# Moving 24 conditioning columns of the first attention to TensorE, with a third load buffer and new scheduling priorities

## The chip, the cores and the metric

The kernel runs on one core of a Trainium2 chip. A core has five engines that work side by side, each on its own instructions in their written order: TensorE (PE; PEld is its weight load), VectorE (DVE), ScalarE (ACT), GpSimd (POOL) and SyncE (SP), which here only issues transfers. The metric is the time of one execution in microseconds (us), the median of several runs; lower is better.

## What is computed

Two transformer layers over 512 tokens of 1024 features, in float32. Both layers are steered by a conditioning vector `c`: a product with a 1024 x 6144 matrix gives six vectors of 1024 per layer (a shift, a scale and a gate for the attention, the same for the MLP). Cut to what matters:

```python
c_act = silu(c)
for l in range(2):
    ada = c_act @ ada_w[l] + ada_b[l]                 # 6 x 1024 numbers
    sh1, sc1, g1, sh2, sc2, g2 = split(ada, 6)
    h = x * (1 + sc1) + sh1
    y = even_mixer(h) if l == 0 else diff_mixer(h)    # attention
    x = layer_norm(ALPHA * x + (1 + g1) * y)
    h = x * (1 + sc2) + sh2
    x = layer_norm(ALPHA * x + (1 + g2) * square(relu(h @ w1)) @ w2)
```

The first attention (`even_mixer`) has two groups of heads: eight with three branches (compressed, selected and window keys; below, the first heads), and eight on a latent of rank 128 with an index that keeps 256 keys for each query (the second heads). The conditioning of layer 0 is 48 columns of 128 numbers: columns 0 to 15 are needed before the first projection, 16 to 23 (the gate `g1`) before the output projection, 24 to 39 before the MLP, 40 to 47 at its end.

## The kernel before

All weights pass through one stream (`Stream`, from L107): a list of items in the order of their use. `issue` (L134) starts the transfer of the next item as soon as a raw buffer of 128 x 1024 floats is free. There are two such buffers for the whole program (`raw0`, `raw1`), four more at the start (`early`, two of them for the first 24 items only) and four in the MLPs. `prepare` then splits a weight into a high part (a rounding copy on ScalarE, L265) and the rest (a subtraction, L266, on DVE or POOL as the table `PLAN` says), since a product is made of three fast matmuls (`mm3`, L350 to L352). A raw buffer comes free when its item is prepared. The table's row `ord` gives the order of the items in the first attention; an `'a'` in it is one conditioning column.

A conditioning column in columns 0 to 39 of layer 0 is 128 outputs on the partitions by 1024 inputs: it is multiplied by `cact`, which holds the activated vector in every partition, and summed along the row. Columns 0 to 15 and three others do that in one DVE instruction (L250); the other 21 do the product on POOL (L247) and the sum on ScalarE (L248). `ada_bias` (L407) then adds the bias to eight columns on DVE. From column 40 on, and in layer 1, two columns come as a pair (`ada_pair`, L416): eight matmuls with 32 columns of weights each (L422), a copy by ScalarE (L425), two sums by a matmul with a selector (L427) and one addition on DVE (L428). A pair keeps its first raw buffer until the second is there, and one of the two PSUM banks of its tag ("mm" in the attention).

The first attention runs in slots. After the first projection (to about 71 us) the slots below 15 project further queries and keys, score the index (L504 and L505 on PE, a relu by ScalarE L1208, an accumulation by DVE L1164), normalise the latent (`latent`, L1102 to L1106 on DVE) and transpose it (`latent_t`, L1113 on PE). Then come 32 units of the first heads: scores (L504, L505), a maximum on DVE (L514), the exponential on ScalarE (L517), scaling on POOL (L1284), transposes (L1486), and the value products with the compressed part (`pv`, L1304 and L1312). Beside them DVE picks the largest index scores (L1190, L1191). Projections fill the gaps by estimated cost (`Fill`). The units of the second heads and the output projection follow.

The order on each engine is not the written one: a scheduler of the framework plays the program with its own durations and takes what is ready. `ahead(n)` raises the priority of what is made inside it, and `ahead(None)` gives it the highest there is; before, only the layer norms use it, with 0.

## Time and profile before

| | us |
|---|---|
| median of 3 runs | 1440.21 (1439.06 to 1440.84) |
| profiled execution | 1441.48 |
| its span, first to last instruction | 1439.40 |
| PE busy in it | 1338.4 |
| DVE busy in it | 1141.7 |
| ACT busy in it | 659.8 |
| POOL busy in it | 579.8 |

The span is what the trace shows; the execution's own time is 2.08 us more. Times of the trace count from the start of the span. The first attention takes about the first 372 us, the first MLP follows until about 800 us, the second attention until about 1065 us, and the second MLP to the end. A busy engine need not be the one that sets the end, and idle time of an engine costs nothing where others are later. "[idle before <-X]" behind a row names what the engine waited for.

### The profile page before, as it was taken

The page shows a single profiled execution, that of the slowest core. Times are in us where ns is not written, and L with a number is a line of the kernel's source. Part 1 is how long each engine was busy: PE and PEld are TensorE (multiplying, and loading weights), DVE is VectorE, ACT ScalarE, POOL GpSimd, SP SyncE. Part 2 cuts the span into 40 slices and gives each one's busy share as a digit, 9 for nine tenths or more (in the row PEclk, how much of TensorE's full clock was granted, in tenths as well). Part 3 has the DMA queues.
Part 4 walks back from the last instruction along what each step waited for, and adds up shares of the span by engine and source line. Part 5 has one row for each costly group of instructions (what it writes and reads, how often), then busy time and mean ns, then how long its engine had stood idle before and what let it go on. Part 6 is the DMA issues. An engine that isn't in the chain of part 4 may idle for free.

```text
span 1439.4 us, 22546 instructions
## 1 busy us (share of the span) xinstructions
PE 1338.4 (93%) x8286; PEld 1123.1 (78%) x8286; DVE 1141.7 (79%) x2186; ACT 659.8 (46%) x1412; POOL 579.8 (40%) x432
## 2 busy tenths in 40 slices
PE   6979799998899999999999799999979899999985
PEld 4868676676589888888887687887769789999974
DVE  7778979667569778877789925788976997888898
ACT  3555465746365423333332536776565443333321
POOL 1423577626432444444453721124164533122234
PEclk9989999899999999999999999999989999999997
DMA  9834323313731554544542442332450233323311
GB/s 353 288 116 142 116 89 118 119 58 118 263 117 46 175 191 162 183 169 161 191 161 94 144 164 88 103 103 76 152 163 6 91 100 118 106 72 117 117 59 59
DMA packets 58657, 189.52 MB, mean 132 GB/s; under 512 B 7794, under 2 KB 8498, under 8 KB 58548
## 3 DMA queue, kind: packets, MB, share of 16 engines
q1 hardware_dynamic: 55840, 184.67, 38.0%
q10 hardware_dynamic: 2708, 3.42, 0.7%
q8 instruction: 65, 1.06, 0.3%
q14 instruction: 44, 0.36, 0.1%
HBM read 178.42 MB, written 9.64 MB: 131 GB/s over the span
## 4 chain that ended last, share of the span: by engine, by line
PE 70%; DVE 19%; DMA 4%; issue 3%; ACT 2%; POOL 1%; DVEq 0%; SPq 0%; ACTq 0%; POOLq 0%
PE ps_mm L350 9%; PE ps_mm L351 9%; PE ps_mm L352 9%; PE ps_o L350 4%; PE ps_o L351 4%; PE ps_o L352 4%; PE ps_s L351 3%; PE ps_s L350 3%; PE ps_s L352 3%; PE ps_t L350 2%; PE ps_t L352 2%; PE ps_t L351 2%; PE ps_t L1486 2%; PE ps_s L504 2%; DVE u L738 2%
## 5 line engine op out<-in xcount | busy, mean ns | idle before, releaser
L350 PE MATMUL ps_mm<-hT,b 128*128 128x256 f32 (+1 forms) x560 | 188.9, 339 | 16.9 <-ACT b L265 13.2
L351 PE MATMUL ps_mm<-hT,b 128*128 128x256 f32 (+1 forms) x560 | 188.5, 337 | 5.2 <-DVE hT L724 5.1
L352 PE MATMUL ps_mm<-hT,b 128*128 128x256 f32 (+1 forms) x560 | 187.8, 336 | 1.8 <-DVE b L220 1.8
L350 PEld LDWEIGHTS ps_mm<-hT,b 128*128 128x128 f32 x560 | 107.6, 192 | 31.9 <-ACT b L265 13.2
L351 PEld LDWEIGHTS ps_mm<-hT,b 128*128 128x128 f32 x560 | 107.8, 193 | 17.8 <-DVE hT L724 5.6
L220 POOL TENSOR_TENSOR b<-s,b 128x512 fp32r<-128x512 f32 x33 | 46.6, 1415 | 184.6 <-ACT b L219 181.2
L517 ACT ACTIVATE z<-z,st 128x128 f32<-128x128 f32 (+3 forms) x160 | 89.3, 559 | 67.2 <-DVE st L514 61.3
L903 POOL TENSOR_TENSOR ot<-z,ot 128x512 fp32r<-128x512 f32 x39 | 61.3, 1573 | 142.0 <-ACT ot L902 128.4
L352 PEld LDWEIGHTS ps_mm<-hT,b 128*128 128x128 f32 x560 | 107.5, 192 | 11.4 <-DVE b L220 2.0
L350 PE MATMUL ps_o<-b,ot 128*128 128x512 f32 x251 | 101.2, 403 | 3.9 <-ACT b L265 2.2
L351 PE MATMUL ps_o<-b,ot 128*128 128x512 f32 x251 | 99.5, 397 | 3.0 <-DVE b L266 3.0
L738 DVE TENSOR_TENSOR u<-ps_o,u 128x512 f32<-128x512 f32 x121 | 82.4, 681 | 21.6 <-PE ps_o L352 21.2
L352 PE MATMUL ps_o<-b,ot 128*128 128x512 f32 x251 | 98.8, 394 | 0.0
L514 DVE CUSTOM_DVE_ANT_0 z<-ps_s,g 128x128 f32<-128x128 f32 (+3 forms) x160 | 75.0, 484 | 25.8 <-PE ps_s L505 23.6
L265 ACT CAST b<-raw 128x1024 fp32r<-128x1024 f32 (+1 forms) x62 | 64.5, 1043 | 65.9 <-issue 16.7
L266 DVE TENSOR_TENSOR b<-s,b 128x1024 fp32r<-128x1024 f32 x47 | 70.4, 1501 | 18.3 <-ACT b L265 17.9
L265 ACT CAST b<-s 128x1024 fp32r<-128x1024 f32 x47 | 49.1, 1049 | 77.6 <-DMA s<-mlp_w 18.9
L266 DVE TENSOR_TENSOR b<-raw,b 128x1024 fp32r<-128x1024 f32 (+1 forms) x42 | 56.7, 1349 | 33.1 <-ACT b L265 32.9
L350 PE MATMUL ps_s<-b,ot 128*128 128x512 f32 x181 | 72.4, 400 | 0.0
L738 DVE TENSOR_TENSOR u<-ps_s,u 128x512 f32<-128x512 f32 x87 | 59.3, 682 | 15.9 <-PE ps_s L352 15.6
L351 PE MATMUL ps_s<-b,ot 128*128 128x512 f32 x181 | 71.7, 396 | 0.0
L352 PE MATMUL ps_s<-b,ot 128*128 128x512 f32 x181 | 71.4, 394 | 0.0
(472 smaller groups left out, 4244.1 us busy)
## 6 DMA issues: line engine op xcount, KB each, us to landing
s<-mlp_w SPq DMA_DIRECT2D x55, 512.0 KB
s<-ada_p SPq DMA_DIRECT2D x39, 512.0 KB
s<-mlp_wp SPq DMA_DIRECT2D x33, 512.0 KB
raw<-ada_w SPq DMA_DIRECT2D x23, 512.0 KB
raw<-mlp_w SPq DMA_DIRECT2D x21, 512.0 KB
raw<-mlp_wp SPq DMA_DIRECT2D x19, 512.0 KB
early<-ada_w SPq DMA_DIRECT2D x17, 512.0 KB
raw<-ada_p SPq DMA_DIRECT2D x17, 512.0 KB
```

Of the source, the lines that this page charges most:

```text
L220: (nc.gpsimd if PLAN["sl"][it.l][n] else nc.vector).tensor_tensor(out=lo, in0=src, in1=f32(hi), op=ALU.subtract)
L265: nc.scalar.copy(out=hi.cols(c.start, w), in_=raw[:, c])
L266: getattr(nc, ("vector", "gpsimd")[PLAN["lo"][it.name]] if it.name in PLAN["lo"] else k.lo_engine).tensor_sub(out=lo.cols(c.start, w), in0 ...
L350: mm(ps, lhsT=l[0], rhs=r[0], start=start, stop=False)
L351: mm(ps, lhsT=l[0], rhs=r[1], start=False, stop=False)
L352: mm(ps, lhsT=l[1], rhs=r[0], start=False, stop=stop)
L504: mm(ps, lhsT=q[:, qs], rhs=k[0][:, ks], start=start, stop=False)
L514: i = nc.vector.tensor_tensor_reduce(out=z[:, :w], in0=ps, in1=bias, scale=-1.0, scalar=3e38, op0=ALU.add, op1=ALU.min, accum_out=st[:, m: ...
L517: j = nc.scalar.activation(out=z[:, :w], in_=z[:, :w], func=AF.Exp, scale=-1.0, bias=st[:, m:m + 1], accum_out=st[:, 2 + m:3 + m])
L738: self.nc.vector.tensor_add(out=u[:, sl], in0=ps, in1=u[:, sl])
L903: (nc.gpsimd if PLAN["hl"][l][f % 2] else nc.vector).tensor_tensor(out=hl[:, c0:c1], in0=r[:, c0:c1], in1=f32(hh[:, c0:c1]), op=ALU.subtract)
L1486: self.nc.tensor.transpose(t[:, 128 * j:128 * j + 128], z[:, 128 * j:128 * j + 128], self.ident)
```

## The change

Columns 16 to 39 of layer 0, 24 of them, become 12 pairs on TensorE; columns 0 to 15 all stay on DVE. With them go L247, L248 and `ada_bias`, since a pair adds the bias itself. A third raw buffer is there for the whole program. Its room comes from `cact`, which now lies in the buffer of the gate row (tag `grow`) and is read last by column 15. The eight matmuls of every pair (all 40) and the value products of the first heads are made inside `ahead(None)`. In `ord` the columns 16 and 17 now come right after `iq`, and 22 and 23 after the first compression weight.

```diff
 PLAN = {...
- 'ax': ((0, 19), (0, 36), (0, 38)),
...
- 'ord': ('iq', 'a', 'ks', 'n0', 'a', 'kw', 'a', 'a', 'a', 'a', 'kc', 'vc', 0, 'a', 1, 2, 3, 'n1', 4, 5, 'a', 6, 7,
+ 'ord': ('iq', 'a', 'a', 'ks', 'n0', 'kw', 'a', 'a', 'a', 'a', 'kc', 'vc', 0, 'a', 'a', 1, 2, 3, 'n1', 4, 5, 6, 7,
          'n2', 'n3'),
...
             if not k.ada_pe(l, m):
-                acc = k.adac[:, l, m:m + 1]
-                if bool(16 <= m < 48) != ((l, m) in PLAN["ax"]):
-                    nc.gpsimd.tensor_tensor(out=raw, in0=raw, in1=k.cact, op=ALU.mult)
-                    nc.scalar.activation(out=raw, in_=raw, func=AF.Copy, scale=0.5, accum_out=acc)
-                else:
-                    nc.vector.scalar_tensor_tensor(out=raw, in0=raw, scalar=0.5, in1=k.cact, op0=ALU.mult,
-                                                   op1=ALU.mult, accum_out=acc)
+                nc.vector.scalar_tensor_tensor(out=raw, in0=raw, scalar=0.5, in1=k.cact, op0=ALU.mult,
+                                               op1=ALU.mult, accum_out=k.adac[:, l, m:m + 1])
             elif m % 2:
                 k.ada_pair(l, m - 1, self.held.raw[0], raw)
...
     def ada_pe(self, l, m):
 
-        return l > 0 or m >= 40
+        return l > 0 or m >= 16
...
     def ada_pair(self, l, m, r0, r1):
...
-        for k in range(8):
-            j = k % 4
-            mm(ps[32 * j:32 * j + 32, :256], lhsT=self.ccol[:, 1, k:k + 1].to_broadcast([128, 32]), rhs=(r0, r1)[k // 4][:, 256 * j:256 * j + 256],
-               start=k < 4, stop=k >= 4)
+        with self.ahead(None):
+            for k in range(8):
+                j = k % 4
+                mm(ps[32 * j:32 * j + 32, :256], lhsT=self.ccol[:, 1, k:k + 1].to_broadcast([128, 32]), rhs=(r0, r1)[k // 4][:, 256 * j:256 * j + 256],
+                   start=k < 4, stop=k >= 4)
...
-        self.cact = C.tile([128, 1024], F32, name="cact")
+        self.cact = self.B.tile([128, 1024], F32, tag="grow", bufs=1, name="cact")
...
         def pv(n):
...
+            with self.ahead(None):
+                for br in range(2):
+                    for j in range(i + 1):
+                        for ab in range(2):
+                            nc.tensor.matmul(o[ab], lhsT=V[:, br, j, 64 * ab:64 * ab + 64], rhs=pts[ab][br][:, 128 * j:128 * j + 128],
+                                             start=i % 2 == 0 and br == 0 and j == 0, stop=False)
...
-                self.ada_bias(0, 2)
...
-            self.ada_bias(0, m)
...
-            for s in range(2):
+            for s in range(3):
                 st.raws.append((self.W.tile([128, 1024], F32, name=f"raw{s}"), 1 << 30))
```

In the changed file the lines above L400 stand some six to nine lower: L413 there is L422 here, L418 is L427, L419 is L428, L495 and L496 are L504 and L505, L1104 is L1113, L1097 is L1106, L1296 is L1304 and L1304 is L1312.

On PE, behind the first projection, before: score units of the index (`ps_s`) around the transposes of the latent (`ps_t`).

```order
L352 MATMUL ps_mm_620<-hT_111,b41_86 128x512
L504 MATMUL ps_s_574<-q_486,ot_491 128x512
L505 MATMUL ps_s_574<-q_487,ot_491 128x512
L504 MATMUL ps_s_614<-q_486,ot_496 128x512
L505 MATMUL ps_s_614<-q_487,ot_496 128x512
L1113 MATMUL ps_t_897<-ident_130,ot_514 128x128 x3
L504 MATMUL ps_s_633<-q_486,ot_497 128x512
L505 MATMUL ps_s_633<-q_487,ot_497 128x512
L1113 MATMUL ps_t_897<-ident_130,ot_514 128x128
```

The same place of the changed program, with conditioning pairs (`ccol`, `sel`) between:

```order
L346 MATMUL ps_mm_632<-hT_113,b41_87 128x512
L1104 MATMUL ps_t_945<-ident_132,ot_516 128x128 x4
L418 MATMUL ps_mm_660<-sel_137,z_669 128x1 x2
L495 MATMUL ps_s_743<-q_488,ot_595 128x512
L496 MATMUL ps_s_743<-q_489,ot_595 128x512
L413 MATMUL ps_mm_693<-raw2_77,ccol_123 32x256 x4
L413 MATMUL ps_mm_693<-early_90,ccol_123 32x256 x4
L418 MATMUL ps_mm_693<-sel_137,z_702 128x1 x2
```

The transposes now come after all of the six first score units and after the matmuls of two pairs; the third pair follows one unit later.

On DVE, the chain that ends in the scaled latent (`ss`, `yi`, `t`, `rk`, then L1106), before:

```order
L473 SCALAR_TENSOR_TENSOR ot_503<-ps_s_180,ot_503 64x512
L250 SCALAR_TENSOR_TENSOR raw1_76,adac_124<-raw1_76,cact_115 128x1024
L1102 TENSOR_SCALAR ss_511<-ss_511 128x4
L1100 TENSOR_SCALAR gates_509<-gates_509 128x96
L384 TENSOR_SCALAR yi_544<-ss_511 128x4
L1101 RECIPROCAL gates_509<-gates_509 128x96
L391 TENSOR_TENSOR t_546<-yi_544 128x4
```

And in the changed program, where L1093 is the former L1102 and L1155 (an index accumulation) the former L1164:

```order
L1155 SCALAR_TENSOR_TENSOR ot_537<-z_629,iw_512,ot_537 128x512
L464 SCALAR_TENSOR_TENSOR ot_596<-ps_mm_560,ot_596 64x512
L1093 TENSOR_SCALAR ss_513<-ss_513 128x4
L419 TENSOR_TENSOR adac_126<-ps_mm_601,adab_125 128x2
L1091 TENSOR_SCALAR gates_511<-gates_511 128x96
L1155 SCALAR_TENSOR_TENSOR ot_537<-z_648,iw_512,ot_537 128x512
L378 TENSOR_SCALAR yi_546<-ss_513 128x4
L1092 RECIPROCAL gates_511<-gates_511 128x96
L385 TENSOR_TENSOR t_548<-yi_546 128x4
```

The column is gone, the addition of the first pair and two index accumulations stand in the chain.

On PE among the units of the first heads, at the start of the last of their four groups (value products `V`), before:

```order
L1486 MATMUL ps_t<-ident,z 128x128 x2
L504 MATMUL ps_s<-k,q 128x128
L505 MATMUL ps_s<-kl,q 128x128
L1259 MATMUL ps_t<-ident,z 128x128
L1304 MATMUL ps_o<-s_2267,V 64x128
L1304 MATMUL ps_o<-s_2204,V 64x128
L1304 MATMUL ps_o<-s_2267,V 64x128
L1304 MATMUL ps_o<-s_2204,V 64x128
L504 MATMUL ps_s<-k,q 128x128
L505 MATMUL ps_s<-kl,q 128x128
```

And in the changed program, with the eighth of the twelve pairs:

```order
L1476 MATMUL ps_t<-ident,z 128x128 x3
L1304 MATMUL ps_o<-ot 64x256 x2
L1296 MATMUL ps_o<-s_2384,V 64x128
L495 MATMUL ps_s<-k,q 128x128
L496 MATMUL ps_s<-kl,q 128x128
L495 MATMUL ps_s<-k,q 128x128
L496 MATMUL ps_s<-kl,q 128x128
L413 MATMUL ps_mm<-raw_77,ccol 32x256 x4
L413 MATMUL ps_mm<-raw_76,ccol 32x256 x4
```

Before, four value products part the scores of one unit from those of its second branch; in the changed piece none does, and a pair stands whole behind the scores. Over all of PE the 160 value products stand in 38 runs, where they stood in 44.

## Rows read from the trace of the kernel before

**Rows 1.** The page's first table: engine, busy us, share of the span, instructions.

```profile
PE 1338.4 (93%) x8286; PEld 1123.1 (78%) x8286; DVE 1141.7 (79%) x2186; ACT 659.8 (46%) x1412; POOL 579.8 (40%) x432
```

**Rows 2.** Stretches: length, busy us of each engine, granted clock, DMA share, GB/s.

```profile
57.00:100.00 43.00, 33.42 (x138) 26.74 (x137) 32.26 (x55) 26.04 (x58) 20.44 (x10) 0.88 0.57 185
140.00:180.00 40.00, 32.72 (x226) 24.68 (x223) 37.81 (x110) 19.23 (x46) 22.57 (x21) 0.91 0.38 125
180.00:300.00 120.00, 115.39 (x780) 85.24 (x779) 91.85 (x287) 74.37 (x196) 83.41 (x75) 0.91 0.34 106
```

**Rows 3.** Waits of PE from 57 to 300 us: total us, times, longest.

```profile
PE ps_s L504 <- DVE st L514: 10.0, 4, 4.0
PE ps_t L1113 <- DVE ot L1106: 7.6, 1, 7.6
PE ps_mm L350 <- DVE ot L473: 2.0, 1, 2.0
```

**Rows 4.** Timeline of DVE around 70 us: start, us, line and operation.

```profile
66.94 3.09 DVE L250 SCALAR_TENSOR_TENSOR raw<-raw,cact 128x1024 f32<-128x1024 f32 x1 [0.19 <-DMA raw<-ada_w]
...
69.95 2.35 DVE L1102 TENSOR_SCALAR ss<-ss 128x4 f32<-128x4 f32 x1
...
72.33 2.31 DVE L384 TENSOR_SCALAR yi<-ss 128x4 int32<-128x4 int32 x1
...
75.22 1.74 DVE L391 TENSOR_TENSOR t<-yi 128x4 f32<-128x4 f32 x1
76.99 0.16 DVE L392 TENSOR_TENSOR t<-t,ss 128x4 f32<-128x4 f32 x1
```

**Rows 5.** Timeline of POOL in the same time.

```profile
68.89 5.72 POOL L247 TENSOR_TENSOR early<-early,cact 128x1024 f32<-128x1024 f32 x2
74.59 2.35 POOL L266 TENSOR_TENSOR b<-raw,b 128x1024 fp32r<-128x1024 f32 x1
```

**Rows 6.** Line L247 on raw buffers: shortest, median, longest ns.

```profile
L247 POOL TENSOR_TENSOR raw<-raw,cact x16: 2352/2390/2544, 66.5 to 290.9; 128x1024 f32<-128x1024 f32 x16
```

**Rows 7.** Timeline of PE around a pair of the first MLP.

```profile
490.88 0.40 PE L350 MATMUL ps_s<-b,ot 128*128 128x512 f32 x1
...
491.34 0.40 PE L352 MATMUL ps_s<-b,ot 128*128 128x512 f32 x1
491.67 1.07 PE L422 MATMUL ps_s<-s,ccol 128*32 128x256 f32 x16
492.67 0.39 PE L350 MATMUL ps_t<-hT,b 128*128 128x256 f32 x1
...
496.52 0.50 PE L427 MATMUL ps_s<-sel,z 128*128 128x1 f32 x4
496.88 0.36 PE L352 MATMUL ps_t<-q,b 128*128 128x256 f32 x1
```

**Rows 8.** Timeline of DVE from 142 to 166 us.

```profile
151.88 2.77 DVE L1164 SCALAR_TENSOR_TENSOR ot<-z,iw,ot 128x384 f32<-128x384 f32 x1
...
160.55 2.56 DVE L1164 SCALAR_TENSOR_TENSOR ot<-z,iw,ot 128x384 f32<-128x384 f32 x1
```

**Rows 9.** DVE and PE near 245 us, and the 20 us stretch around.

```profile
242.25 2.33 DVE L407 TENSOR_TENSOR adac<-adac,adab 128x8 f32<-128x8 f32 x1
...
245.84 0.47 PE L504 MATMUL ps_s<-k,q 128*128 128x128 f32 x1 [1.87 <-DVE st L514]
...
240.00:260.00 20.00, 18.09 (x105) 13.38 (x103) 14.75 (x47) 11.70 (x33) 15.69 (x14) 0.74 0.36 97
```

**Rows 10.** Chain that ended last, pieces of value products: start, us, records.

```profile
193.92 1.89 PE ps_o L1304 x30
197.00 0.36 PE ps_o L1304 x2
```

**Rows 11.** Waits of PE from 300 to 372 us.

```profile
PE ps_o L1435 <- DVE s L529: 2.2, 2, 1.4
PE ps_t L1486 <- DVE s L529: 2.1, 2, 1.8
```

14 lines of the change are left out of this document (3 added, 11 removed).

## The prediction

> **What bounds the kernel now.** I read the page's busy shares first, then a table of stretches of the first attention, then the waits of TensorE (PE) there, and last the timelines around the longest of these waits. PE is busy 93% of the span [rows 1]; so an instruction put on PE has to find a hole in PE or it lengthens the run. The holes in the first attention are few and lie early: PE is busy 33.42 of the 43 us from 57 to 100, 32.72 of 40 from 140 to 180, and 115.39 of 120 from 180 to 300 [rows 2]. From 57 to 300 the waits of PE that a semaphore ended are nearly all for DVE: 10.0 us for the softmax maximum of L514, 7.6 us for the scaled latent of L1106, 2.0 us for an index query of L473 [rows 3]. From 140 to 180 DVE itself is busy 37.81 of 40: there DVE is the bound, and from 180 to 300 it is PE. [...]
>
> Why DVE is late shows in the rows around 67 us. A conditioning column on DVE (L250) takes 3.09 us, then L1102 takes 2.35, L384 2.31 and L391 1.74 on four columns each, where L392 on the same shape takes 0.16 [rows 4]. In the same 10 us POOL runs two conditioning products back to back (5.72 us) and then one L266 [rows 5]. Small DVE operations stretch while POOL runs a big one. [...]
>
> **The change part by part.** Removed: 21 columns on POOL and ScalarE (16 of them on raw buffers, where the product takes 2.39 us on POOL [rows 6]), three on DVE, and three additions of the bias. In their place stand 12 pairs on TensorE, each with one copy on ScalarE and one tiny addition on DVE.
>
> Price of a pair, from the pairs that the MLP already runs [rows 7]. Its eight matmuls make 16 records between an L352 that starts at 491.34 and an L350 that starts at 492.67. Of these 1.33 us the L352 takes 0.23 anyway (490.88 to 491.34 is two such steps), so 1.10 are the pair's. The two sums with the selector start at 496.52 and the next matmul at 496.88: 0.36. Together 1.46 us, twelve pairs 17.5 us, all in the first attention.
>
> *57 to 140.* In the changed order four pairs stand here: +5.8. The latent's transposes (L1113 before) come after the matmuls of two pairs and after six score units, of which three stood behind them before. DVE loses L250 (3.09), and since both products beside them go, L1102 and L384 lose their stretch (2.35 + 2.31 less two of 0.16, so 4.3): together 7.4 of the 7.6 us wait. L391's stretch stood beside an L266, which stays; I count nothing for it. PE arrives later besides, so -7.6. The 2.0 us wait on L473 is the same backlog a few us later: -2.0. Clock: 0.12 of 43 us are 5.2 us of clock lost, part of it while PE stood still; I take -3.0 (0 to -5.2). What is late next: the score units stand in bursts on PE now and share two PSUM banks, so each waits until ScalarE has read the one before the last; and on DVE the first pair's addition, which waits for PE and for ScalarE's copy, now stands ahead of the chain that ends in L1106. I take +3.0 for both, between nothing and the 4.0 us of the longest wait for DVE that PE has here [rows 3]. Sum -3.8, between -9.0 and +2.2.
>
> *140 to 180.* PE's long waits for L514 lie here, the longest 4.0 [rows 3]. Ahead of the L514 that ends it DVE runs an L1164 of 2.56 us, and ahead of the other one an L1164 of 2.77 [rows 8]; both ran beside an L266 of POOL, which the change keeps. For a gain: DVE enters this stretch with some 7 us less behind it. I take -3.0, between 0 and -7.3, since the order shifts which operations meet. [...]
>
> *180 to 300.* Eight pairs: +11.7. Gone is POOL's conditioning product between the softmax scalings, and with it an addition of the bias (L407) that took 2.33 us; PE then waited 1.87 us until 245.84, and the granted clock of the 20 us around is 0.74 [rows 9]. PE's idle time here sums to 4.6 us (120 less 115.39), of which I take back 3. A clock of 0.91 in 120 us is 10.8 us lost at most; nothing here shows that added pairs lift it, but the waits that precede its falls partly go: I take -4. Value products: 30 records in one run take 1.89 us, 63 ns each, two in a run 0.36 [rows 10], so a run costs 0.23 beside its records. The order has 38 runs instead of 44: -1.4. Sum +3.3, between +11.7 and -5.1 (all idle time, all clock, the runs).
>
> *300 to 372 and later.* PE waits 2.2 and 2.1 us here for copies of L529 on DVE [rows 11]. The third raw buffer lets one more output weight lie ready, and DVE meets less of POOL: -1.5, between +1 (a pair holds two of three buffers until its second column has come) and -4.3. The MLPs and the second attention keep their instructions; the 28 later pairs already stand mostly in one run. I cost them at nothing, hidden in the dense matmul stream; if their order turned worse it would be PE time one to one.
>
> The POOL and ScalarE time of the 21 columns counts for nothing by itself: from 180 to 300 POOL is busy 83.41 and ScalarE 74.37 of 120 [rows 2]. Moving the conditioning vector into the gate row's buffer costs nothing: its last reader is column 15, done before the gate row is written.
>
> Sum: -3.8 - 3.0 + 3.3 - 1.5 = -5.0. The profiled execution took 1441.48 us, 2.08 more than its span of 1439.40 and 1.27 more than the median of 1440.21. So 1441.5 - 5.0 - 1.3 = 1435.2.
>
> **The rivals.** *TensorE has slack.* The 115.39 us are the union of records whose ends are modelled; weight loads fill 85.24 of the 120 us [rows 2], and between records of different width there are gaps into which a pair may fit. Then the eight pairs cost nothing from 180 to 300, and that term is -8.4 instead of +3.3: 1435.2 - 11.7 = 1423.5. For it: the low share of weight loads. Against it: the 1.10 us of a pair came on top in full between the dense rows of the MLP. [...]
>
> *TensorE ends last everywhere.* From 140 on the pairs are paid in full, the clock gives nothing back, and DVE's stretches beside L266 stay: the term of 140 to 180 is 0 and that of 180 to 300 is 11.7 - 1.4 = +10.3. Then -3.8 + 10.3 - 1.5 = +5.0, so 1441.5 + 5.0 - 1.3 = 1445.2, slower. It decides when what waits and clock give back from 140 to 300 stays below about 5 us. For it: PE's 96% there. Against: PE's low clock around 245 follows a wait for DVE.
>
> *The buffer does not do what its name says.* A pair keeps two of the three raw buffers and one of two PSUM banks, so loads and projections come no earlier: the last term is +1, and the new waits from 57 to 140 are 4 instead of 3. That is 3.5 worse than the forecast: 1438.7, no change.
>
> **How the numbers follow.** Chances: the forecast 0.42, slack 0.16, no change 0.16, TensorE last 0.26. Measurements of this kernel tell about 0.2% (2.9 us) from no change. Faster 0.42 + 0.16 = 0.58, same 0.16, slower 0.26. The likeliest case alone covers 1428 to 1437. All bounds together reach from 1414 to 1455; to hold 8 in 10 the range runs from 1418, half of its 11 us beyond the slack rival, to 1448, 3 us beyond the slower one.
>
> **What would show it.** Right: no wait of PE over 2 us for the latent's transposes; DVE's operations of L1102 and L384 near 0.2 us; a pair of 1.1 us; a granted clock above 0.91 from 140 to 300; the last value product no later than before. Wrong: PE's busy time up by the whole 17.5 us and the end of the value products later by as much (TensorE last), or that end over 10 us earlier (slack). New waits of PE for ScalarE's copy of a pair, or for a PSUM bank among the score units, would show the part of 57 to 140 that I guessed.

## The result: the changed kernel is slower

The changed kernel takes 1450.4 us (median of five runs, 1447.7 to 1455.6) where the kernel before takes 1440.2: a ratio of 1.0075, 95% interval 1.0051 to 1.0099, about 10 us slower. A second set of runs gave 1449.0 us and a ratio of 1.0061 (1.0038 to 1.0084). The forecast was 1435.2, and the range ended at 1448. The profiled execution of the changed kernel took 1448.5 us with a span of 1446.7.

The first table of its page, against [rows 1]:

```profile
PE 1354.4 (94%) x8526; PEld 1129.1 (78%) x8526; DVE 1131.4 (78%) x2189; ACT 640.3 (44%) x1382; POOL 523.3 (36%) x411
```

PE has 16 us more, POOL 57 us less. The three stretches of [rows 2], after (length, busy us of PE, PEld, DVE, ACT, POOL, granted clock, DMA share, GB/s):

```profile
57.00:100.00 43.00, 36.51 (x193) 25.72 (x191) 23.05 (x46) 20.80 (x50) 7.38 (x4) 0.88 0.51 167
140.00:180.00 40.00, 36.98 (x321) 28.43 (x321) 38.53 (x123) 21.09 (x53) 21.88 (x21) 1.00 0.39 124
180.00:300.00 120.00, 112.91 (x903) 80.96 (x903) 86.90 (x288) 62.51 (x174) 49.55 (x64) 1.00 0.34 107
```

The waits of PE from 57 to 300 us, after, against [rows 3]. The wait of 7.6 us for the latent is gone, that for the softmax maximum (L514 before, L505 after) has fallen from 10.0 to 2.4, and a new one stands first, for ScalarE's copy of a pair (L416):

```profile
PE ps_mm L418 <- ACT z L416: 2.6, 2, 2.1
PE ps_s L495 <- DVE st L505: 2.4, 2, 1.3
PE ps_t L1476 <- DVE s L520: 2.2, 2, 1.5
```

Read like this, the change did most of what the prediction hoped for, and yet the time went up. Where it went shows when the span is cut at marks that both kernels have: the transposes of the LayerNorms (L713 before, L704 after). The first of them starts at 372.4 us before, near the end of the first attention; the last one of the same cluster starts at 418.0, behind the output projection; then come the first MLP, its end, the second attention with its output projection, and the last MLP. The six stretches of the kernel before, in the columns just given:

```profile
0.00:372.40 372.40, 327.91 (x2046) 253.23 (x2047) 291.12 (x757) 202.57 (x478) 180.16 (x162) 0.94 0.46 154
372.40:418.00 45.60, 41.81 (x278) 34.48 (x279) 30.10 (x53) 19.23 (x46) 23.14 (x17) 0.89 0.66 228
418.00:797.60 379.60, 375.75 (x2553) 320.26 (x2552) 304.26 (x437) 137.51 (x244) 156.53 (x100) 1.00 0.41 146
797.60:823.90 26.30, 17.79 (x82) 14.18 (x81) 25.33 (x36) 13.72 (x32) 22.41 (x14) 0.87 0.49 161
823.90:1082.40 258.50, 241.45 (x1276) 203.22 (x1275) 184.39 (x470) 161.62 (x401) 75.59 (x61) 0.97 0.39 123
1082.40:1439.40 357.00, 333.64 (x2058) 297.77 (x2056) 306.52 (x436) 125.12 (x216) 122.01 (x80) 0.98 0.25 85
```

and the same six of the changed kernel:

```profile
0.00:376.00 376.00, 341.85 (x2307) 256.45 (x2308) 280.51 (x760) 184.34 (x448) 129.14 (x142) 0.99 0.47 156
376.00:416.80 40.80, 37.29 (x261) 31.83 (x259) 29.45 (x52) 19.26 (x46) 21.91 (x16) 0.92 0.69 246
416.80:797.00 380.20, 375.85 (x2552) 319.70 (x2551) 304.85 (x437) 136.88 (x243) 151.46 (x100) 1.00 0.42 146
797.00:823.10 26.10, 17.53 (x83) 14.24 (x82) 25.20 (x36) 13.47 (x32) 22.33 (x14) 0.80 0.52 155
823.10:1090.90 267.80, 247.06 (x1278) 207.39 (x1277) 183.98 (x471) 161.62 (x401) 75.51 (x62) 0.95 0.37 119
1090.90:1446.70 355.80, 334.87 (x2057) 299.50 (x2055) 307.38 (x436) 124.72 (x216) 122.96 (x80) 0.98 0.25 83
```

Three stretches moved. The first attention to its first LayerNorm transpose is 3.6 us longer; its end is 4.8 us shorter (45.6 to 40.8); and the second attention, in which no instruction was changed, is 9.3 us longer (258.5 to 267.8). The sum of the first four stretches is even: the end of the first MLP comes 0.8 us earlier than before. In this execution the whole loss stands in the second attention, behind the last edited instructions: the last pair's matmuls (L413) start at 741.5 us.

One execution must not be trusted for the first stretch: over the study's profiles of kernels with the same first attention it ended at 375.7, 376.0, 381.1 and 382.2. A part of that stands at the very start: the 96th record of the three projection lines (L344 to L346 after), in the first projection, which no edit touches, starts at 40.6 us here, at 45.1 in a second profile of the same kernel (e6), and at 38.9 in the kernel before. Where first stretches are compared below, they are also counted from that record. The other stretches repeat within about 4 us where the order is the same: the second attention in its old order took 258.1 to 262.6 us in the study's profiles.

The second attention's end, on PE's timeline (start, us, line, operation, idle time before it). Before:

```profile
1050.24 1.03 PE L713 MATMUL ps_t<-ident,ot 128*128 128x128 f32 x8
...
1053.86 1.03 PE L713 MATMUL ps_t<-ident,ot 128*128 128x128 f32 x8
1061.81 1.11 PE L713 MATMUL ps_t<-ident,ot 128*128 128x128 f32 x4 [6.92 <-ACT ot L719]
```

After:

```profile
1059.02 1.03 PE L704 MATMUL ps_t<-ident,ot 128*128 128x128 f32 x8
1068.24 1.12 PE L704 MATMUL ps_t<-ident,ot 128*128 128x128 f32 x4 [8.19 <-ACT ot L710]
1072.49 0.58 PE L344 MATMUL ps_mm<-hT,b 128*128 128x256 f32 x1 [1.74 <-ACT hT L714]
```

Before, 12 matmuls of the output projection stand between the first row block's transposes (1050.24) and the second's (1053.86). After, the first block's stand at nearly the same time (from 1051.4), but 24 matmuls follow ahead of the second block's at 1059.02. Less is left then to cover the LayerNorm of the last blocks: PE waits 8.19 us instead of 6.92, and the granted clock is 0.50 there for 17.0 us (1064.1 to 1081.1) where before it was 0.50 for 13.7 (1058.0 to 1071.7). This end is the smaller part of the loss: from the second block's transposes on it takes 31.9 us instead of 28.5. The rest, 5.9 us, stands ahead of them, before and after:

```profile
823.90:1053.90 230.00, 222.18 (x1145) 184.88 (x1144) 164.93 (x444) 142.33 (x359) 59.28 (x51) 1.00 0.36 115
823.10:1059.00 235.90, 226.38 (x1145) 188.06 (x1144) 165.50 (x443) 144.00 (x362) 63.29 (x54) 0.98 0.35 115
```

The same 1145 records are 4.2 us longer busy, and the granted clock is 0.50 there for 10.2 us (1002.6 to 1006.0 and 1036.8 to 1043.6) where the kernel before has no such stretch (1.00 over all of it). The program's order of the second attention differs from about its last third on, though no line of it was edited; what made it differ is the first question.

### The profile page after: what moved, and what is told of

Read it like the earlier page. It is cut to its first block, busy times and chain, and to the rows that moved or that the text cites. A ratio compares the mean times of both kernels' runs of the same rounds, so it can differ in the third digit from the quotient of the medians.

```text
span 1446.7 us, 22958 instructions
## 1 busy us (share of the span) xinstructions
PE 1354.4 (94%) x8526; PEld 1129.1 (78%) x8526; DVE 1131.4 (78%) x2189; ACT 640.3 (44%) x1382; POOL 523.3 (36%) x411
## 4 chain that ended last, share of the span: by engine, by line
PE 73%; DVE 17%; ACT 3%; DMA 3%; issue 2%; POOL 2%; SPq 0%; DVEq 0%; ACTq 0%; POOLq 0%
PE ps_mm L344 10%; PE ps_mm L345 9%; PE ps_mm L346 9%; PE ps_o L345 4%; PE ps_o L344 4%; PE ps_o L346 4%; PE ps_s L345 4%; PE ps_s L344 3%; PE ps_s L346 3%; PE ps_t L344 2%; PE ps_t L345 2%; PE ps_t L346 2%; PE ps_t L1476 2%; DVE u L729 2%; DVE b L260 2%
## 5 line engine op out<-in xcount | busy, mean ns | idle before, releaser
L344 PE MATMUL ps_mm<-hT,b 128*128 128x256 f32 (+1 forms) x560 | 188.8, 340 | 19.6 <-ACT b L259 14.4
L346 PE MATMUL ps_mm<-hT,b 128*128 128x256 f32 (+1 forms) x560 | 188.2, 337 | 1.8 <-DVE b L219 1.8
L344 PEld LDWEIGHTS ps_mm<-hT,b 128*128 128x128 f32 x560 | 108.1, 193 | 33.6 <-ACT b L259 14.4
L894 POOL TENSOR_TENSOR ot<-z,ot 128x512 fp32r<-128x512 f32 x39 | 57.6, 1478 | 165.2 <-ACT ot L893 151.6
L346 PEld LDWEIGHTS ps_mm<-hT,b 128*128 128x128 f32 x560 | 108.1, 193 | 11.1 <-DVE b L219 2.0
L259 ACT CAST b<-raw 128x1024 fp32r<-128x1024 f32 (+1 forms) x78 | 81.0, 1046 | 76.6 <-POOL raw L256 18.6
L260 DVE TENSOR_TENSOR b<-raw,b 128x1024 fp32r<-128x1024 f32 (+1 forms) x55 | 76.3, 1391 | 40.2 <-ACT b L259 39.8
L344 PE MATMUL ps_o<-b,ot 128*128 128x512 f32 x251 | 99.4, 396 | 1.4 <-DVE u L729 1.2
L260 POOL TENSOR_TENSOR b<-raw,b 128x1024 fp32r<-128x1024 f32 x23 | 54.9, 2390 | 120.5 <-ACT b L259 106.0
L346 PE MATMUL ps_o<-b,ot 128*128 128x512 f32 x251 | 98.3, 392 | 0.0
L505 DVE CUSTOM_DVE_ANT_0 z<-ps_s,g 128x128 f32<-128x128 f32 (+3 forms) x160 | 75.3, 485 | 22.7 <-PE ps_s L496 19.1
L219 POOL TENSOR_TENSOR b<-raw,b 128x512 fp32r<-128x512 f32 x25 | 35.7, 1429 | 136.0 <-ACT b L218 128.8
L344 PE MATMUL ps_s<-b,ot 128*128 128x512 f32 x181 | 72.4, 400 | 0.1
L346 PE MATMUL ps_s<-b,ot 128*128 128x512 f32 x181 | 71.9, 397 | 0.0
L893 ACT CAST ot<-z 128x512 fp32r<-128x512 f32 x52 | 32.2, 620 | 89.3 <-DVE z L909 57.3
```

The source lines that it names most:

```text
L219: (nc.gpsimd if PLAN["sl"][it.l][n] else nc.vector).tensor_tensor(out=lo, in0=src, in1=f32(hi), op=ALU.subtract)
L259: nc.scalar.copy(out=hi.cols(c.start, w), in_=raw[:, c])
L260: getattr(nc, ("vector", "gpsimd")[PLAN["lo"][it.name]] if it.name in PLAN["lo"] else k.lo_engine).tensor_sub(out=lo.cols(c.start, w), in0 ...
L344: mm(ps, lhsT=l[0], rhs=r[0], start=start, stop=False)
L346: mm(ps, lhsT=l[1], rhs=r[0], start=False, stop=stop)
L505: i = nc.vector.tensor_tensor_reduce(out=z[:, :w], in0=ps, in1=bias, scale=-1.0, scalar=3e38, op0=ALU.add, op1=ALU.min, accum_out=st[:, m: ...
```

## Experiments

Each compares with the kernel before in the same session. Times are medians; the ratio is to the kernel before with its 95% interval. Where us are worked out from ratios, 0.1% is 1.44 us. Executions of one kernel lie up to 15 us apart here, so differences below 3 us between two runs are not read. e7, e8, e14 and e15 leave out work that the result needs; they serve as measures alone.

### Is it the third buffer in the second attention?

**e1.** In the changed kernel the third raw buffer is dropped when the stream comes to the second attention's first block.

```diff
-                st.raws.append((self.W.tile(..., name=f"raw{s}"), 1 << 30))
+                st.raws.append([self.W.tile(..., name=f"raw{s}"), 1 << 30])
+            self.third = st.raws[2]
...
         o2, its = self.even() if l == 0 else self.odd()
+        if l == 0:
+            self.third[1] = st.items.index(self.I1["v", 0, 0])
```

> The changed kernel, but the third raw buffer is dropped when the stream reaches the second attention's first weight block: the first attention's order on TensorE is that of the changed kernel word for word, the second attention's that of the kernel before. Theory A (the loss is the second attention's end, whose order the third buffer changes: the last transposes of its LayerNorm start 8.5 us later than in the kernel before, while those of the first MLP's end start 0.7 us earlier): about 1440, that is 1438 to 1443, and within 0.3% of the kernel before; the last L713-line transposes before the last MLP near 1082 us. Rival B (the loss is the 17.5 us of the twelve pairs on TensorE, which somewhere become time one to one): stays near 1450, 1447 to 1454.

Measured: 1446.2 us, ratio 1.004 (1.002 to 1.006). The second attention's stretch is 258.5 us, as the theory said; the time is between the two expectations. The buffer is dropped inside the first MLP already. In the profiled execution, the slowest of its twelve, that MLP took 385.1 us and its end 27.8, against 380.2 and 26.1, but 381.5 and 381.8 us in e4 and e7, which drop the buffer at the same place. That the early drop costs something is not shown; e9 tries a later one.

**e5.** The reverse: the kernel before gets a third buffer from the second attention on (the tile of the conditioning factor, dead by then).

```diff
+        if l == 1:
+            st.raws.append((self.cact, 1 << 30))
         o2, its = self.even() if l == 0 else self.odd()
```

> The kernel before, whose conditioning factor (the tile that the 24 columns were multiplied with, dead after the first attention) becomes a third raw buffer from the second attention on. The first attention has the order of the kernel before, the second attention word for word that of the changed kernel. Theory A2 (the third buffer's order of the second attention costs 4 to 9 us by itself): 1445 to 1450, and the stretch from the last LayerNorm transpose of the first MLP's end to the last one of the second attention's end takes 263 to 268 us against 258.5 before. Rival: the long second attention of the changed kernel's profile was one execution's half-clock stretch, and the time is 1440 to 1442, the stretch 257 to 261 us.

Measured: 1447.6 us, ratio 1.0046 (1.0022 to 1.0071). The second attention's stretch:

```profile
824.00:1092.10 268.10, 245.84 (x1280) 206.44 (x1278) 184.84 (x470) 161.56 (x401) 74.41 (x61) 0.96 0.36 117
```

268.1 us instead of 258.5, with the last MLP 1.5 us shorter. One buffer more, no other edit, and 6.6 us are lost (3.2 to 10.2 by the interval). **e6** is the changed kernel again.

> The changed kernel itself, beside the others on one chip and for a second profile. Theory A2: the stretch of the second attention takes 265 to 270 us again, the first attention ends (first LayerNorm transpose) at 376 to 382 us. Rival: the stretch takes 258 to 261 us and the loss stands before 380 us. Time near 1450 for both.

Measured: 1449.0 us; first LayerNorm transpose at 382.2, second attention 267.7 us. The second attention's loss is there again, and the first attention, which ended at 376.0 in the first profile, is longer here, 4.5 us of it in the start.

**e9.** The buffer is dropped later than in e1, at the second attention's output weights (`self.I1["oo", 0]` in place of `self.I1["v", 0, 0]`).

> The changed kernel, its third raw buffer dropped where the stream comes to the second attention's first output weights (later than in the first experiment, which dropped it inside the first MLP). TensorE's order is that of the changed kernel word for word to the end of the first MLP but for some 30 places, then that of the kernel before. Theory A2 (the third buffer costs 9 us in the second attention's end, gives 1 back in the last MLP, and dropped inside the first MLP it costs 2 to 5 there): 1440 to 1443, second attention's stretch 258 to 259 us. Rival (the first experiment's 1446 was all that can be had by it): 1445 to 1448.

Measured: 1446.2 us, ratio 1.0037 (1.0014 to 1.0059), as e1. The stretch is back at 260.9 us; the time is 3 us under e6, at the rival's value and not at 1440 to 1443. The stretches of this run: 375.7, 40.0, 382.8, 25.9, 260.9, 357.4; the MLP's 2 us more and the last MLP's 1.6 take a part. So theory A2 is right on the place and explains only part of the loss: 5 us are left with the second attention in its old order.

### What is the third buffer worth elsewhere?

**e2.** The changed kernel with two raw buffers (`range(2)` for `range(3)`).

> The changed kernel with two raw buffers from the start to the end, all else as changed. Its second attention has the order of the kernel before but for two or three matmuls. Theory A: the 8 to 9 us of the second attention's end come back; the first attention, whose pairs now take both raw buffers while they wait, loses between 0 and 8 us of it: 1440 to 1449. Rival B: 1450 or more. Rival C (a pair without a third buffer stalls the stream for most of its transfer, 12 pairs by 1 to 2 us): 1453 to 1465.

Measured: 1450.1 us, ratio 1.0078 (1.0055 to 1.0101): rival B's value, though not for its reason. The second attention is back at 258.0 us, but the first attention's end takes 46.2 us, as in the kernel before, where the changed kernel has 40.8. Against e9, which has the third buffer until the second attention's output weights, two buffers cost 5.9 us (1.0078 less 1.0037).

**e12.** The kernel before; its dead conditioning tile becomes a third raw buffer after the last of the 24 columns, until the second attention's output weights.

```diff
             self.raws.append(it.raw)
+            if it.ada == (0, 39):
+                self.raws.append((self.k.cact, self.items.index(self.k.I1["oo", 0])))
```

> The kernel before, with the columns on VectorE and GpSimd as they were, whose conditioning factor's tile becomes a third raw buffer as soon as the last of the 24 columns is done, and is dropped at the second attention's first output weights. Its second attention has the order of the kernel before. Theory H (the stretch from the first attention's end to its last LayerNorm transpose takes 40 to 41 us with a third buffer and 45.6 to 47 without it): that stretch 40 to 42 us and the time 4 to 6 us under the kernel before, 1434 to 1437. Rival (those 5 us come from the columns that were taken off VectorE, or are lost again in the first MLP): within 2 us of 1440.

Measured: 1430.8 us, ratio 0.9933 (0.9907 to 0.9959), 3 us better than the better expectation. Its second and fifth stretch:

```profile
364.30:404.40 40.10, 36.30 (x260) 30.74 (x259) 28.85 (x52) 19.26 (x46) 22.54 (x16) 0.96 0.69 240
...
810.80:1071.30 260.50, 242.85 (x1277) 204.10 (x1276) 185.47 (x471) 161.94 (x401) 76.00 (x62) 0.97 0.38 121
```

The first attention's end takes 40.1 us instead of 45.6. This part of the change is a gain of 9.6 us that needs no column moved: the buffer came free in the kernel before as well.

### What are the pairs worth, and the columns that they replace?

**e7.** e1 without the twelve pairs.

```diff
         nc, mm = self.nc, self.nc.tensor.matmul
+        if l == 0 and m < 40:
+            nc.vector.tensor_copy(out=self.adac[:, l, m:m + 2], in_=self.adab[:, l, m:m + 2])
+            return
         ps = self.bank(self.ada_tag)
```

> The changed kernel with the third buffer dropped at the second attention, as in the first experiment, and the twelve pairs of the first attention left out: their 24 columns are loaded, and nothing is computed from them. Theory B2 (the pairs' 17.5 us of TensorE are worth 60 to 100 per cent in the time): 11 to 17 us under the first experiment's 1446, that is 1429 to 1435. Rival (TensorE has slack there): within 4 us of 1446.

Measured: 1423.4 us, ratio 0.9884 (0.9852 to 0.9915). The pairs are worth 22.5 us (1.004 less 0.9884), more than the 17.5 that they take on PE.

**e8.** The kernel before without the 24 columns.

```diff
                 acc = k.adac[:, l, m:m + 1]
-                if bool(16 <= m < 48) != ((l, m) in PLAN["ax"]):
+                if m >= 16:
+                    nc.vector.memset(acc, 0.0)
+                elif bool(16 <= m < 48) != ((l, m) in PLAN["ax"]):
```

> The kernel before with the same 24 columns loaded and not computed: no multiplication and no sum of them on VectorE, GpSimd and ScalarE. Prediction's theory (these steps of 4.6 to 8 us each held up the chains that TensorE waits for): 8 to 14 us under the kernel before, 1427 to 1432. Theory B2 (they lay beside TensorE's work, so that taking them away frees little, and the pairs replaced a cheap thing by a dear one): 1436 to 1440. The difference of this run from the one without pairs is what the change's other parts (order of loads, priorities, a buffer of the first attention) are worth.

Measured: 1422.0 us, ratio 0.9877 (0.9852 to 0.9903): 17.7 us, above both expectations. The prediction was right that the columns on VectorE and GpSimd held up TensorE. But 17.7 is all there was to gain, and the pairs cost 22.5 in the changed kernel.

**e10.** e9 with each of the twelve pairs' eight matmuls issued twice.

```diff
-            for k in range(8):
+            for k in 2 * tuple(range(8)) if l == 0 and m < 40 else range(8):
```

> The kernel of the run before this one (third buffer to the output weights), in which each of the first attention's twelve pairs issues its eight matmuls twice: 96 matmuls more, 12 x 1.10 = 13.2 us of TensorE. Theory B3 (TensorE's time is one to one there): 11 to 15 us above that kernel. Rival F (the pairs' 23 us are mostly their chain: the copy, the selector sums, the addition, and the waits for them): under 7 us above it.

Measured: 1453.1 us, ratio 1.0084 (1.0056 to 1.0112): 6.8 us above e9 for 13.2 us of TensorE: just rival F. About half of the added time is swallowed; by the two intervals it may be anything from a little to most of it.

**e14.** e9 with the pairs' matmuls alone.

```diff
+        if l == 0 and m < 40:
+            nc.vector.tensor_copy(out=self.adac[:, l, m:m + 2], in_=ps[:, :2])
+            return
         s = self.z()[:, :256]
         nc.scalar.copy(out=s, in_=ps[:, :256])
```

> The same kernel with third buffer to the output weights, whose twelve pairs of the first attention issue their eight matmuls and nothing more: ScalarE's copy, the two selector sums and the addition are left out, and one VectorE copy of two columns out of PSUM stands in their place. Rival F (what a pair costs is mostly the chain behind it): 9 to 14 us under that kernel, 1432 to 1437. Theory B3 (it is the matmuls, 13.2 of the 17.5 us of TensorE): 3 to 6 us under it.

Measured: 1422.9 us, ratio 0.9869 (0.9841 to 0.9897): 24 us under e9, further than rival F went, and not above e7, which has no pair at all. Where the chain behind them (ScalarE's copy, two selector sums, VectorE's addition) is left out, the matmuls of twelve pairs cost nothing that can be measured; putting the chain back costs 24 us. Whether the matmuls are as cheap beside the chain is another matter: e10 says about half. From the 96th projection record to the first LayerNorm transpose, e7 without pairs, e14 with the matmuls, and e9 with the chain too:

```profile
48.90:361.40 312.50, 297.87 (x1963) 229.70 (x1962) 240.49 (x685) 165.87 (x419) 119.94 (x126) 0.96 0.42 140
43.00:357.30 314.30, 304.28 (x2155) 227.56 (x2154) 244.38 (x707) 167.29 (x421) 122.61 (x126) 0.99 0.45 142
39.30:375.70 336.40, 317.82 (x2203) 238.00 (x2202) 251.29 (x707) 172.22 (x433) 122.55 (x126) 0.98 0.42 133
```

From e7 to e14 PE has 192 records more, 6.4 us more busy time and 4.6 us less idle time, at a granted clock of 0.99 instead of 0.96: 1.8 us in all. From e14 to e9 the stretch grows by 22.1 us, 13.5 of them PE's busy time (the 48 records of selector sums are 7.1) and 8.6 idle. How long a pair keeps its PSUM bank shows in the first pair of the changed kernel, from its first matmul to its addition (four rows of the timeline, PE, ACT, PE and DVE):

```profile
66.17 1.07 PE L413 MATMUL ps_mm<-raw,ccol 128*32 128x256 f32 x16
...
72.53 0.39 ACT L416 COPY z<-ps_mm 128x256 f32<-128x256 f32 x1
...
73.74 0.85 PE L418 MATMUL ps_mm<-sel,z 128*128 128x1 f32 x4
...
76.55 0.16 DVE L419 TENSOR_TENSOR adac<-ps_mm,adab 128x2 f32<-128x2 f32 x1
```

and in the first pair of e14:

```profile
68.59 1.07 PE L413 MATMUL ps_mm<-raw,ccol 128*32 128x256 f32 x16
...
70.67 0.16 DVE L416 COPY adac<-ps_mm 128x2 f32<-128x2 f32 x1
```

10.5 us against 2.2. One of the two banks of the tag that the projections use too is away for so long, while the copy queues on ScalarE behind a rounding copy, a copy of a projection and a relu of index scores, and the addition on VectorE behind two index accumulations. Over the twelve pairs, the time in which at least one stands between its first matmul and its addition sums to 86 us in e9 and 37 in e14. That sum alone does not set the time: in e13 (below) it is 102 us, and e13 is 11.9 us faster than e9.

### The priorities

**e3.** The kernel before with the value products' priority alone (`with self.ahead(None):` around the loop of the diff).

> The kernel before with one part of the change, the value products' highest priority; conditioning columns, buffers and order of loads as before. Theory D (the priority is what regains the time in 155 to 295 us: in the changed kernel the first value product starts 7.5 us later than before and the last ends 4 us earlier): 1428 to 1436, the last value product at about 288 to 292 us against 299 in the kernel before. Rival E (the regained time comes from the vector engine and GpSimd, which lost the columns, and the priority gives nothing): 1438 to 1442, last value product within 2 us of 299.

Measured: 1441.2 us, ratio 1.0009 (0.999 to 1.0028): rival E, the priority has no worth there. (The last value product came at 293.7 us, and it gained nothing.) **e4** takes it away from e1.

> The first of these kernels (third buffer dropped at the second attention) without the value products' priority. Theory D: the last value product starts 8 to 12 us later than with it (near 304 us against 295) and the time is 6 to 12 us above that of the first kernel, about 1449. Rival E: within 2 us of the first kernel.

Measured: 1449.3 us, ratio 1.0076 (1.0054 to 1.0099), 3 us by the medians and 5 by the ratios above e1: between theories. The intervals of the two overlap, so that the priority gains something beside pairs is not shown. The last value product of e4 stood at 294.5, before e1's 299.7: that mark says nothing on the time. **e11** takes the priority from the pairs of e9.

> The same kernel with the third buffer to the output weights, without the pairs' highest priority (the value products keep theirs). Theory G (the pairs cost more than their 17.5 us since, first in line, they are put ahead of work that others wait for): 3 to 7 us under that kernel. Rival B3 (it is TensorE time wherever it stands): within 2 us of it.

Measured: 1443.0 us, ratio 1.0021 (1.0004 to 1.0038): 3 us under e9 by the medians and 2 by the ratios, at the edge of theory G. The intervals overlap; that a pair which goes first is put ahead of work that others wait for is argued and not shown.

### The order of loads

**e13.** e9 with the kernel before's order of loads.

```diff
- 'ord': ('iq', 'a', 'a', 'ks', 'n0', 'kw', 'a', ..., 0, 'a', 'a', 1, 2, 3, 'n1', 4, 5, 6, 7,
+ 'ord': ('iq', 'a', 'ks', 'n0', 'a', 'kw', 'a', ..., 0, 'a', 1, 2, 3, 'n1', 4, 5, 'a', 6, 7,
```

> The changed kernel with the third buffer to the second attention's output weights (1446.2 in the run of that kernel) and the kernel before's order of loads, in which the eight columns 16 to 23 stand among the weights at other places. Theory K (the new order, which loads two columns ahead of the first weights of this stage, holds up the first attention): 3 to 6 us under that kernel, 1440 to 1443. Rival L (the order was fitted to pairs and helps them): 2 to 6 us above it.

Measured: 1434.8 us, ratio 0.9954 (0.993 to 0.9977): 11.9 us under e9, twice what theory K gave, and faster than the kernel before. Not one instruction is added or left out. **e15** does the same without pairs.

> The same kernel with the kernel before's order of loads and the twelve pairs left out (loaded, not computed). The run without pairs and with the new order gave 1423.4. Theory K: 3 to 6 us less than that, 1417 to 1420. Theory M (the loss without pairs is the pairing itself: a raw buffer is held until its partner has come, which the order doesn't change): within 2 us of 1423.

Measured: 1412.5 us, ratio 0.9794 (0.9766 to 0.9821): 13 us under e7. So the order is worth the same without pairs; it is not about them.

Where it shows first: the compression's matmuls (L1534 before, L1524 after) begin behind 112 matmuls on each of the three projection lines in every kernel. With the new order 13 score units and four pairs stand ahead of them too; with the old one 14 or 15 score units and three pairs (in e13 also half of the fourth's matmuls). The stretch from 57 us to that begin, in the changed kernel, in e13 and in e18 (below), which has the old order too:

```profile
57.00:119.30 62.30, 54.74 (x274) 40.41 (x273) 41.77 (x84) 29.31 (x65) 10.11 (x6) 0.92 0.44 146
```

```profile
57.00:111.40 54.40, 52.17 (x277) 40.09 (x275) 40.53 (x83) 27.45 (x64) 7.78 (x5) 1.00 0.49 154
```

```profile
57.00:107.80 50.80, 49.02 (x253) 37.63 (x251) 43.50 (x94) 27.52 (x64) 7.72 (x5) 0.97 0.47 145
```

With the new order the compression begins at 119.3 us (124.6 in e6, 116.4 in e9), with the old one at 111.4 and 107.8; PE stands idle 7.6 us of the stretch instead of 2.2 and 1.8, at a granted clock of 0.92 instead of 1.00 and 0.97. Counted from the 96th projection record it is 78.7 us (79.5 and 77.1) against 67.9 and 68.0, with one pair less. The kernel before begins the compression at 110.2 without any pair, 71.3 from that record. The waits of PE there in e9, whose counterparts in e13 are all 0.9 us or less:

```profile
PE ps_s L495 <- DVE ot L464: 1.8, 2, 1.4
PE ps_mm L418 <- ACT z L416: 1.7, 2, 1.3
PE ps_s L495 <- ACT z L1199: 1.4, 1, 1.4
```

With two columns loaded in a row the first pair comes early, and the weights `ks` and `n0` come one load later; in the rows pairs, index queries and score units then meet in a bunch. That this bunch is the cause was not tried apart from the order, and two runs speak against its being all: e2, with the new order and two raw buffers, begins the compression at 112.4 (73.0 from the record) and is no faster than the changed kernel; and without pairs the old order makes this part 4.4 us shorter (64.7 in e7, 60.3 in e15), of 12.3 us up to the first LayerNorm transpose (312.5 and 300.2). What the order changes behind the compression was not traced. In e13's own profile the granted clock is 0.96 from 180 to 240 us and 0.87 from 240 to 300, where e17 and e18 (below) have 1.00 in both; that execution took 1443.3 us, the slowest but one of its twelve.

### Can the pair's chain be had cheaper?

**e17.** e13, the copy written into the pair's own raw buffer.

```diff
-        s = self.z()[:, :256]
+        s = r1[:, :256] if l == 0 and m < 40 else self.z()[:, :256]
```

> The changed kernel with the old load order and the third buffer to the second attention's output weights (1434.8 in the run of that kernel); the copy of each of the first attention's twelve pairs goes into the pair's own second raw buffer, which its matmuls have just read, and no longer into one of the eleven rotating buffers that the score units use. Theory Z (the chain costs 23 us because it takes these buffers): 8 to 15 us under 1434.8, 1420 to 1427. Rival P (it costs as TensorE time of the selector sums, as ScalarE time and by the PSUM bank that it holds): 1432 to 1438.

Measured: 1434.9 us, ratio 0.9953 (0.9931 to 0.9975), the same as e13: by this the rotating buffers that pairs share with the score units are not the matter, unless a gain was hidden by the raw buffer, which each pair now keeps until its selector sums. What is left of the chain's price is the bank, ScalarE's place in the queue and the selector sums; these were not separated. **e18** is e17 without the pairs' priority.

> The kernel of the run before this one without the pairs' highest priority. Theory G (the priority costs 3 us wherever it stands): 2 to 5 us under that run. Rival: within 2 us of it. Under 1430.8 it is the fastest kernel of the study that computes everything.

Measured: 1429.6 us, ratio 0.9916 (0.9884 to 0.9948): the fastest of the kernels that compute everything, 0.8% faster than the kernel before. **e16** is e12 with the value products' priority.

> The kernel before with its dead conditioning tile as third raw buffer between the last column and the second attention's output weights (1430.8), and the value products' highest priority besides. If the priority has a worth of its own (3 us between two of the runs with pairs): 1426 to 1429. If it has none, as on the kernel before alone (1441.2 against 1440.6): 1430 to 1432.

Measured: 1432.0 us, ratio 0.9937 (0.9912 to 0.9961): as e12, the priority shows no worth without pairs. e12, e16 and e18 can't be told apart by their intervals. e12 keeps the columns where they were and e18 has them on TensorE: once the load order, the buffer and the priority are put right, moving them is worth nothing that these runs can tell.

## Why the prediction was wrong

**The signs came out right, the time did not.** The prediction named five things that would show its steps right. All five hold in the profile: PE does not wait for the latent's transposes any more, the two small operations that took 2.35 and 2.31 us [rows 4] (L1102 and L384 before) take 0.17 and 0.16, as DVE's timeline of the changed kernel shows,

```profile
76.34 0.17 DVE L1093 TENSOR_SCALAR ss<-ss 128x4 f32<-128x4 f32 x1
...
77.40 0.16 DVE L378 TENSOR_SCALAR yi<-ss 128x4 int32<-128x4 int32 x1
```

a pair's matmuls take 1.07 us, the clock from 140 to 300 is 1.00, and the last value product (L1296 after, shown as first and last start) comes at 294.4 against 298.5:

```profile
L1296 PE MATMUL ps_o<-s,V x320: 272/273/324, 165.7 to 294.4; 128*64 128x128 f32 x160
```

Each of them shows a cost removed, and the mark of the value products is no mark of the time, as e3 and e4 showed; in e6, the same kernel, it stands at 300.8. The one sign that the prediction named for the costs it guessed, new waits of PE for ScalarE's copy of a pair, showed too, with 2.6 us in all, and told nothing of the 22.5 us that the pairs cost. Of its signs of being wrong, PE's busy time rose by 16.0 of the 17.5 us while the value products did not come later.

**The failing step: two parts priced at nothing.** The sum has no term for the order of loads, which the prediction read as a part of placing four pairs; it is the largest single loss, 12 us (e9 against e13, and 13 without pairs). And of the second attention it says "I cost them at nothing": the third buffer alone costs 6.6 us there (e5; 3.5 to 5.5 by taking it away again, e9 against the two ratios of the changed kernel), since a stretch without an edited instruction was set in a new order, which can only be priced by reading that order. The prediction saw the risk (PE time one to one) and gave it neither a place nor a chance. e13 is the changed kernel without these two parts, and it took 1434.8 us where the forecast was 1435.2. That it came so near is partly luck, since the terms that are left miss in both directions.

**Pairs for columns, -2.1 foreseen.** The prediction paid 20.5 us for the pairs (17.5 on PE and 3.0 for new waits) and took 22.6 back for the columns (7.6, 2.0 and 3.0 in 57 to 140, 3.0 in 140 to 180, 3 and 4 in 180 to 300). Measured, 17.7 came back (e8) and 22.5 were paid (e7 against e1): +4.8. The removal was right in its cause and put too high by a quarter. The price was nearly right in size and of another kind: the matmuls, 1.10 of the 1.46 us, cost nothing without their chain (e14), and the chain 24 us for twelve, so the likeliest case and the rival "TensorE ends last everywhere" both priced mostly the part that can be free. The prediction named the chain's ingredients, the wait for ScalarE's copy, the second PSUM bank, the addition ahead of others on DVE, and gave them 3.0 us in 57 to 140 and nothing later. From the row of a pair alone this could have been seen: the selector sums of [rows 7] start 3.8 us behind the matmuls' end, even in the MLP, where few others wait.

**57 to 140, -3.8.** It was outside its bounds: the compression begins 9.1 us later (7.4 counted from the 96th projection record), with 5.8 of pairs. The waits that were to go went; with the new order of loads others came. Of the 3.0 us of clock that were to come back nothing shows: the granted clock from 57 to 100 is 0.88 after as before.

**140 to 180, -3.0.** Right in the direction on PE (36.98 busy of 40 against 32.72, clock 1.00 against 0.91), though DVE stays as full as before (38.53 against 37.81). Before, the two index accumulations of 2.77 and 2.56 us [rows 8] ran beside an L266 (L260 after) of POOL, of 2.36 and 2.37 us (from 151.88 and 160.33). In the changed kernel these two operations hardly meet here: the six index accumulations that begin between 140 and 180 us take 0.60 to 0.82 us, none of them beside an L260. The next one runs beside an L260 on POOL (181.85, for 2.44 us) and is long again, 1.72 us; the longest of the six and this one:

```profile
153.82 0.82 DVE L1155 SCALAR_TENSOR_TENSOR ot<-z,iw,ot 128x384 f32<-128x384 f32 x1
...
182.98 1.72 DVE L1155 SCALAR_TENSOR_TENSOR ot<-z,iw,ot 128x384 f32<-128x384 f32 x1
```

**180 to 300, +3.3.** From the first value product (158.2, 165.7 after) to the last, 140.3 us before and 128.7 after, with seven pairs more in it; the eighth starts at 301.4. The rival "TensorE has slack" was right on this in part: matmuls can go in for nothing (e14, 1422.9 us against 1423.4 without pairs), but the second set of e10 cost 6.8 of its 13.2 us. That PE was busy 115.39 of 120 us before did not keep the matmuls of e14 from going in (with them it was busy 304.28 of 314.30 us). For the clock the prediction took back 4 us; the granted clock went from 0.91 to 1.00, and what that gave in time no run shows by itself.

**300 to 372 and later, -1.5.** The third buffer's gain was there and mis-sized: 9.6 us in the kernel before (e12), 5.5 of it behind 372 in the first attention's output projection (45.6 to 40.1 us), and 5.9 beside pairs (e2 against e9).

**The sum.** Exchange +5, load order +12, third buffer -9.6 or -5.9 and +6.6, the value products' priority beside pairs between 0 and -5 (not shown to be either): +9 to +18, against 9 to 11 measured. The parts were measured on different kernels, so this is an account and not a proof; the move of the conditioning vector into the gate row's buffer was not run by itself. The rival "TensorE ends last everywhere" has the right sign (1445.2), but its reason, pairs paid in full as TensorE time, is not what the runs show. "The buffer does not do what its name says" does not hold either: the buffer gains in the first attention (e12) and costs in the second (e5).

## What to carry to other kernels

Price a step that you move onto another engine by its chain, from the first instruction that takes a shared resource (here a PSUM bank) to the one that gives it back, and not by the busy time of its largest part: here the chain of twelve pairs cost 24 us (e9 against e14) and their matmuls nothing that can be measured. Where a scheduler or a pool decides the order, a buffer or a load that moves by one place is an edit of every later stretch: compare the order of unedited stretches too, and try each such part by itself, since here a gain of 9.6 us and losses of 12 and 6.6 came in one change. And give a sign for an added cost a size: a wait that merely appears, as the 2.6 us for a pair's copy did here, does not tell what the part costs.

## What was not expected of the hardware

Twelve pairs' matmuls, 192 records, came at no price that can be measured where their chain was left out: in one execution each, 6.4 us of busy time more and 4.6 of idle time less than without pairs, at a granted clock of 0.99 and 0.96. In the kernel before, the granted clock is 0.50 from 245.7 to 255.9 us, where PE had stood idle 1.87 us until 245.84, and from 273.0 to 283.2, behind 1.35 us idle until 271.46. In the changed kernel PE stands idle 1.42 us until 245.72 and 1.30 until 248.83, and the granted clock from 180 to 300 is 1.00. So an idle time of 1.3 to 1.4 us stands ahead of a low clock in one of these traces and not in the other; what brings the clock down is not shown. What is free in one order need not be in another: e10's second set cost 6.8 us for 13.2.
